# Memory tokens and key weights in eight joint pieces, compressed-value products 512 wide, and a new order table, in a decoder block of sparse attention, mLSTM and memory attention

## The chip, the cores and the metric

The kernel runs on one core of a Trainium2 chip. The metric is the time of one execution on the device in microseconds (us); where several executions were timed it is their median. A profile is one execution, taken by the hardware profiler. The engines are called TensorE (PE in the rows, its weight loads PEld), VectorE (DVE), ScalarE (ACT), GpSimd (POOL) and SyncE (SP, which here only issues DMAs).

## What is computed

One decoder layer on 256 tokens of 1024 features, in fp32. Cut to what matters here:

```
h = rmsnorm(x, g_pre_mix)
z = h @ w_in          # q_nsa, kv_nsa, gates, qkv_ml, if_ml, o_ml, q_mem, g_merge

# sparse attention: compressed, selected and window branches, 4 groups of 4 heads, 64 wide
o_cmp, p_cmp = nsa_compressed(q, k_cmp, v_cmp, ...)   # softmax over 15 compressed blocks
top_i        = nsa_select(p_cmp)
y_nsa = g0 * o_cmp + g1 * nsa_selected(q, k, v, top_i) + g2 * nsa_window(q, k, v)

y_ml  = sigmoid(o_ml) * headnorm(mlstm_chunkwise(...))

# cross attention to 256 memory tokens
kv    = rmsnorm(mem, g_mem) @ w_mem_kv                # 512 key and 512 value columns
y_mem = softmax(q_mem @ k.T * scale) @ v

y = gm0 * (y_nsa @ w_proj_nsa) + gm1 * (y_ml @ w_proj_ml) + gm2 * (y_mem @ w_proj_mem)
x = x + rmsnorm(y @ w_out, g_post_mix)
h = rmsnorm(x, g_pre_ffn)
x = x + rmsnorm((silu(h @ w_gate) * (h @ w_up)) @ w_ffn_down, g_post_ffn)
```

## The kernel before

**Numbers.** An fp32 product is made from three faster ones. Each operand is split in a high half (rounded by a ScalarE copy, `hi`) and a low half (the remainder, by a VectorE subtraction, `lo`); TensorE adds hi·hi, hi·lo and lo·hi in PSUM. The function `split` is this pair. In the rows `whi` and `wlo` are the halves of a weight unit, `hh` holds those of the normed x, `mh` and `ml` those of the memory tokens.

**Weights.** They stream in units of 128x1024 floats (512 KB), each by one DMA from the stacked tensor `W` into one of four `raw` buffers; `fetch` issues the load, `room` takes buffers for the halves (four each), `split` fills them. The program has 161 units. All loads go through SyncE onto one queue, in the order in which they are issued; a load into a `raw` buffer is issued once that buffer's former content has been read.

**The head.** First come the keys of the memory: 1024 features in eight blocks of 128, by 512 key columns. The array `head` holds the gain of the norm (8 columns), the first block of the transposed memory (256), key unit 0 (1024) and the other seven blocks (1792). Four loads of it (`part`, 776, 768, 512 and 1024 columns) fill the tile `memt`; key units 1 to 3 come from `W` between and behind them. `mem_in(k)` makes `mh` and `ml` of block k. Key units 0 to 2 are split in two halves, unit 3 in one (the constant HEAD). For a block TensorE makes 12 matmuls of 256 columns (rows pd<-mh,whi, pd<-ml,whi and pd<-mh,wlo, four each); eight blocks are 96. After that come four value units of the memory (rows pss<-whi,mh and so on, 48 matmuls of 512 columns), and then the units of the sparse attention's keys and values, called kv units here (pss<-hh,whi, hh,whi and hh,wlo in turn, 24 matmuls of 256 columns each). Before the kv units x must be there: VectorE scales the transposed x (`xt`, eight blocks, loaded in two halves), ScalarE copies the high halves `hh`, VectorE subtracts for the low ones. ScalarE also takes the sums of squares of xN and memN (rows xn and mn); from them come 1/rms, made on GpSimd, and its spread over the partitions by the small matmuls rbc<-cs,rr (for x) and rbc<-cs,rm (for the memory).

**The sparse attention** runs in eight halves (four groups by two blocks of 128 tokens), function `nsa_half`, interleaved with the projections that follow. In each half the compressed probabilities of four heads are transposed together (`ptc`), split (`ch` on ScalarE, `cl` on VectorE), and spread by GpSimd into two tiles `ce` of 128x512, one from `ch`, one from `cl`, which are zero outside each head's own 32 rows. TensorE then multiplies `vcs`, the compressed values, with `ce`, in two pairs of heads with two halves each: four matmuls of 256 columns (L1285 to L1288), added to the sum `pvn`.

**What sets the order.** Every engine call is recorded in a `Plan` and issued at the end. `choose` computes for each operation a rank (how late it may come) with the planner's own costs, lays the operations out in time by rank with `schedule`, and issues each engine's instructions in that order. `EARLY` is a table of operation numbers with nanoseconds by which one operation is made more urgent (or, negative, less). Because all instructions are issued in one helper line, every row of the trace says L618.

Of the kernel before, what the change touches and what calls it, by code (L numbers as in the profile page):

```python
# [11 lines left out]
F32 = mybir.dt.float32  # L12
# [6 lines left out]
P = 128  # L19
S = 256  # L20
D = 1024
KD = D // P
# [4 lines left out]
N_UNITS = 161  # L27
HEAD = (2, 2, 2, 1)
# [139 lines left out]
class Plan:  # L168
# [453 lines left out]
def block_kernel(ctx, tc, order, xN, xT, memN, head, cst, vec, row, wg, w1, w2, W, out):  # L622
# [14 lines left out]
    def bigt(tag, bufs, shape, dt, name):  # L637
        return big.tile(shape, dt, tag=tag, bufs=bufs, name=name)
# [32 lines left out]
    ready = {}  # L671
# [108 lines left out]
    mt = bigt("KK", 1, [P, 3080], F32, "memt")  # L780
    part = lambda a, b: dma(out=mt[:, a:b], in_=head[:, a:b])
# [11 lines left out]
    def mem_in(k):  # L793
        gain = mt[:, k:k + 1]
        src = mt[:, 8:264] if k == 0 else mt[:, 1032 + k * S:1288 + k * S]
        if k == 0:
            DVE.tensor_scalar(mh[:, k, :], src, gain, None, op0=ALU.mult)
        else:
            ACT.activation(mh[:, k, :], src, AF.Copy, scale=gain)
        DVE.scalar_tensor_tensor(ml[:, k, :], src, gain, mh[:, k, :].bitcast(F32),  # L800
                                 op0=ALU.mult, op1=ALU.subtract)
# [9 lines left out]
    part(0, 776)  # L811
    part(776, 1544)
    fetch(("mem_k", 1))
    part(1544, 2056)
    fetch(("mem_k", 2))
    part(2056, 3080)
# [4 lines left out]
    for u in range(4):  # L821
        if u and ("mem_k", u) not in ready:
            fetch(("mem_k", u))
        raw = ready.pop(("mem_k", u)) if u else mt[:, 264:1288]
        w = room()
        pieces = HEAD[u]
        for h in range(2):
            if h < pieces:
                c = slice(1024 // pieces * h, 1024 // pieces * (h + 1))
                split(w[0][:, c], w[1][:, c], raw[:, c])  # L830
            mem_in(2 * u + h)
# [389 lines left out]
    def nsa_half(g, tb, qs, yT):  # L1221
# [63 lines left out]
        for pr in range(2):  # L1285
            for i in range(2):
                PE.matmul(pv[:, 2 * pr:2 * pr + 2, :], vcs[:, g, :], ce[i][:, 2 * pr:2 * pr + 2, :],
                          start=False, stop=(pr == 1 and i == 1), skip_group_check=True)  # L1288
# [173 lines left out]
def _layout(inputs):  # L1462
# [79 lines left out]
    head = np.concatenate([a["g_mem"][0].reshape(KD, P).T, memT[:, 0:S], units["mem_k", 0], memT[:, S:]], axis=1)  # L1542
# [33 lines left out]
```

## Time and profile before

| | |
|---|---|
| time, median of 3 runs | 530.76 us (530.58 to 531.57) |
| time of the profiled execution | 530.48 us |
| its span | 528.7 us |
| mean granted clock of TensorE | 0.999 |
| DMA: bytes, mean rate | 97.69 MB, 185 GB/s |
| ScalarE busy | 348.1 us (66%) |
| weight units loaded | 161 x 512 KB, median 4.1 us from issue to landing |

The span reaches from the first to the last instruction in the trace; 1.78 us of the execution lie around it. A row of a timeline has the start, the length, the engine, the operation as out<-in by the program's tile names, the shape, how many instructions it joins, and in brackets how long the engine stood idle ahead of it and what ended that. Lengths of TensorE rows overlap, since matmuls are pipelined: how long one takes in a sequence is read from the distance between starts.

### The profile page before, as it was taken

How to read it: one execution, taken by the hardware profiler on the slowest of the kernel's cores; microseconds unless marked ns; L12 is line 12 of the kernel's file. 1: busy time of each engine (PE TensorE's matmuls, PEld its weight loads, DVE VectorE, ACT ScalarE, POOL GpSimd, SP SyncE). 2: the span in 40 equal slices, each digit the busy share in tenths (PEclk: the TensorE clock that was granted, in tenths of full speed). 3: DMA queues.
4: the chain of work that ended last, by engine and by line, in shares of the span. 5: the costliest groups of instructions: out<-in, count | busy, mean ns of one | idle time of the engine just before them, and what ended most of it. 6: DMA issues, size and time to landing. Idle time of an engine off the chain costs nothing.

```text
span 528.7 us, 9672 instructions
## 1 busy us (share of the span) xinstructions
PE 520.1 (98%) x3536; PEld 479.3 (91%) x3536; DVE 421.5 (80%) x915; ACT 348.1 (66%) x689; POOL 26.0 (5%) x37
## 2 busy tenths in 40 slices
PE   8999999999999999999999999999999999999995
PEld 8899998989899999999999998888888888888884
DVE  5799898799998989998987888966776877754543
ACT  6887977566887968876995446655555655554531
POOL 0000000010002021111110000000000000000000
PEclk9999999999999999999999999999999999999999
DMA  8995465536443181346364766635554665555512
GB/s 310 417 359 213 141 239 160 199 121 197 152 153 139 45 287 69 121 145 215 124 211 145 219 219 209 229 120 170 190 199 166 195 205 191 200 199 195 182 62 79
DMA packets 28703, 97.69 MB, mean 185 GB/s; under 512 B 3312, under 2 KB 5232, under 8 KB 28400
## 3 DMA queue, kind: packets, MB, share of 16 engines
q1 hardware_dynamic: 28656, 97.07, 53.8%
q8 instruction: 28, 0.46, 0.4%
q14 instruction: 19, 0.16, 0.1%
HBM read 94.96 MB, written 1.05 MB: 182 GB/s over the span
## 4 chain that ended last, share of the span: by engine, by line
PE 95%; DMA 1%; ACT 1%; POOL 1%; issue 1%; DVE 0%; SPq 0%; DVEq 0%; ACTq 0%
PE pd L618 49%; PE pss L618 33%; PE pvn L618 3%; PE sc L618 2%; PE ptn L618 2%; DMA raw<-in_W 1%; POOL ce L618 1%; PE ph L618 1%; PE ptx L618 1%; PE psm L618 1%; PE pn L618 1%; PE pvm L618 1%; PE pq L618 1%; PE pgf L618 0%; DVE z L618 0%
## 5 line engine op out<-in xcount | busy, mean ns | idle before, releaser
L618 ACT ACTIVATE whi<-raw 128x1024 fp32r<-128x1024 f32 (+1 forms) x159 | 165.8, 1050 | 119.8 <-PE pss L618 50.6
L618 DVE TENSOR_TENSOR wlo<-raw,whi 128x1024 fp32r<-128x1024 f32 (+1 forms) x159 | 192.1, 1218 | 64.9 <-ACT whi L618 64.1
L618 PE MATMUL pd<-hh,whi 128*128 128x256 f32 x800 | 148.6, 281 | 0.0
L618 PEld LDWEIGHTS pd<-hh,whi 128*128 128x128 f32 x800 | 124.2, 189 | 0.3
L618 PE MATMUL pd<-hh,wlo 128*128 128x256 f32 x400 | 112.2, 280 | 0.0
L618 PEld LDWEIGHTS pd<-hh,wlo 128*128 128x128 f32 x400 | 75.3, 188 | 0.0
L618 PE MATMUL pss<-xc,whi 128*128 128x512 f32 x168 | 43.3, 392 | 0.0
L618 PE MATMUL pss<-whi,u 128*128 128x512 f32 x132 | 42.0, 390 | 0.0
L618 PEld LDWEIGHTS pss<-xc,whi 128*128 128x128 f32 x168 | 30.5, 188 | 5.2
L618 PE MATMUL pd<-xc,whi 128*128 128x512 f32 x120 | 31.5, 392 | 0.0
L618 PE MATMUL pd<-whi,hh 128*128 128x512 f32 x96 | 31.4, 397 | 0.0
L618 DVE CUSTOM_DVE_ANT_0 sc<-sc,msk 128x16 f32<-128x16 f32 (+2 forms) x96 | 27.1, 316 | 4.0 <-PE sc L618 3.7
L618 PEld LDWEIGHTS pss<-whi,u 128*128 128x128 f32 x132 | 24.8, 188 | 5.2
L618 ACT ACTIVATE pp<-sc,mx 128x128 f32<-128x128 f32 (+1 forms) x64 | 26.7, 428 | 0.1
L618 PE MATMUL pss<-wlo,u 128*128 128x512 f32 x66 | 25.7, 389 | 0.0
L618 PEld LDWEIGHTS pd<-xc,whi 128*128 128x128 f32 x120 | 22.0, 188 | 3.7
L618 PEld LDWEIGHTS pss<-xc,wlo 128*128 128x128 f32 x168 | 22.4, 188 | 1.8
L618 PE MATMUL pss<-xc,wlo 128*128 128x256 f32 x168 | 22.6, 277 | 0.0
L618 PEld LDWEIGHTS pd<-whi,hh 128*128 128x128 f32 x96 | 17.7, 188 | 3.2
L618 DVE TENSOR_SCALAR pp<-pp,sm 128x256 f32<-128x256 f32 (+1 forms) x72 | 19.8, 316 | 0.1
L618 ACT ACTIVATE pTh<-ptn 128x512 fp32r<-128x512 f32 x24 | 13.5, 599 | 9.5 <-PE ptn L618 9.5
L618 PE MATMUL pd<-wlo,hh 128*128 128x512 f32 x48 | 18.9, 394 | 0.0
(328 smaller groups left out, 1068.6 us busy)
## 6 DMA issues: line engine op xcount, KB each, us to landing
raw<-in_W SPq DMA_DIRECT2D x161, 512.0 KB, 4.1
w<-in_w SPq DMA_DIRECT2D x2, 1024.0 KB, 8.3
xn<-in_xN SPq DMA_DIRECT2D x2, 512.0 KB, 10.3
mn<-in_memN SPq DMA_DIRECT2D x2, 512.0 KB, 8.7
xt<-in_xT SPq DMA_DIRECT2D x2, 512.0 KB, 8.7
kk<-kk SPq DMA_DIRECT2D x8, 128.0 KB, 3.1
x<-in_xN SPq DMA_DIRECT2D x2, 512.0 KB, 4.1
memt<-in_head SPq DMA_DIRECT2D x1, 512.0 KB, 7.7
```

The lines of the kernel that those rows point to most:

```text
L618: op.ins_ = getattr(op.real, op.method)(*map(arg, op.a), **{k: arg(x) for k, x in op.kw.items()})
```

## The change

Four edits.

1. The head array is laid out in eight pieces of 768 columns, each a block of the transposed memory (256) and the 512 columns of key weights that belong to it. Pieces 0 and 1 go into `memt`, pieces 2 to 7 into `raw` buffers (named `half`). The key units leave `W`: 158 units remain. Every unit is now split in two halves, so unit 3 has one split pair more. The halves stand 16 columns further in their buffers.
2. In `nsa_half` two matmuls of 512 columns take the place of four of 256, 16 in place of 32 in the program.
3. The table `EARLY` is another one, of 139 entries where there were 109; since operations have gone, its numbers stand for other operations than before.
4. N_UNITS follows.

```diff
-N_UNITS = 161
-HEAD = (2, 2, 2, 1)
+N_UNITS = 158
...
     EARLY = """
-    2:14648000 3:2049450 5:2018550 83:28200 145:2300 149:-2050 150:2350 152:5200 153:6450 160:119500 212:14250
...
+    2:32395300 3:4438550 4:838200 5:282400 6:1428950 7:88800 148:4850 149:93250 150:2050 151:2600 152:2050
...
-    mt = bigt("KK", 1, [P, 3080], F32, "memt")
-    part = lambda a, b: dma(out=mt[:, a:b], in_=head[:, a:b])
+    mt = bigt("KK", 1, [P, 1544], F32, "memt")
...
-        src = mt[:, 8:264] if k == 0 else mt[:, 1032 + k * S:1288 + k * S]
+        src = halves[k][:, 0:S]
...
-    part(0, 776)
-    part(776, 1544)
-    fetch(("mem_k", 1))
-    part(1544, 2056)
-    fetch(("mem_k", 2))
-    part(2056, 3080)
+    halves = [mt[:, 8:776], mt[:, 776:1544]]
+    dma(out=mt[:, 0:776], in_=head[:, 0:776])
+    dma(out=mt[:, 776:1544], in_=head[:, 776:1544])
+    for k in range(2, KD):
+        halves.append(wpool.tile([P, 768], F32, tag="raw", bufs=4, name="half"))
+        dma(out=halves[k], in_=head[:, 8 + 768 * k:776 + 768 * k])
...
     for u in range(4):
-        if u and ("mem_k", u) not in ready:
-            fetch(("mem_k", u))
-        raw = ready.pop(("mem_k", u)) if u else mt[:, 264:1288]
-        w = room()
-        pieces = HEAD[u]
+        w = room((16, 16))
         for h in range(2):
-            if h < pieces:
-                c = slice(1024 // pieces * h, 1024 // pieces * (h + 1))
-                split(w[0][:, c], w[1][:, c], raw[:, c])
+            c = slice(512 * h, 512 * h + 512)
+            split(w[0][:, c], w[1][:, c], halves[2 * u + h][:, S:])
             mem_in(2 * u + h)
...
-        for pr in range(2):
-            for i in range(2):
-                PE.matmul(pv[:, 2 * pr:2 * pr + 2, :], vcs[:, g, :], ce[i][:, 2 * pr:2 * pr + 2, :],
-                          start=False, stop=(pr == 1 and i == 1), skip_group_check=True)
+        for i in range(2):
+            PE.matmul(pv, vcs[:, g, :], ce[i], start=False, stop=i == 1, skip_group_check=True)
```

The table moves instructions on all engines. Three places are shown, before and then after; the issuing line is L618 in the kernel before and L620 in the changed one.

**SyncE, the start of the program**: the loads in the order in which they enter the queue (`raw` are weight units, `mn` memN, `xn` x, `xt` its transpose, `vc` and `cs` constants). Before:

```order
L618 DMA memt<-in_head 128x768
L618 DMA memt<-in_head 128x512
L618 DMA raw<-in_W 128x1024 x2
L618 DMA memt<-in_head 128x1024
L618 DMA raw<-in_W 128x1024 x2
L618 DMA xn<-in_xN 128x1024 x2
...
L618 DMA raw<-in_W 128x1024 x2
L618 DMA mn<-in_memN 128x1024
L618 DMA xt<-in_xT 128x1024
L618 DMA raw<-in_W 128x1024 x2
L618 DMA mn<-in_memN 128x1024
L618 DMA xt<-in_xT 128x1024
```

After:

```order
L620 DMA memt<-in_head 128x776
L620 DMA memt<-in_head 128x768
L620 DMA half<-in_head 128x768 x4
L620 DMA xn<-in_xN 128x1024
L620 DMA half<-in_head 128x768 x2
L620 DMA raw<-in_W 128x1024 x2
L620 DMA xn<-in_xN 128x1024
L620 DMA vc<-in_vec 128x80
L620 DMA cs<-in_cst 128x128
L620 DMA raw<-in_W 128x1024 x3
L620 DMA xt<-in_xT 128x1024 x2
L620 DMA mn<-in_memN 128x1024 x2
```

The first half of x now stands between the pieces, and the first kv unit (the last of `raw` x3) ahead of both transposed halves of x and of memN; the second kv unit comes after them.

**ScalarE and VectorE, from the memory's value units to the second kv unit.** Before, first ScalarE from the second pair of value units on, then VectorE there:

```order
L618 ACTIVATE whi<-raw 128x1024 x2
L618 ACTIVATE mn,sums<-mn 128x1024
L618 ACTIVATE hh<-xt 128x256 x4
L618 ACTIVATE whi<-raw 128x1024 x2
L618 ACTIVATE mn,sums<-mn 128x1024
L618 ACTIVATE hh<-xt 128x256 x4
L618 ACTIVATE whi<-raw 128x1024 x2
```

```order
L618 SCALAR_TENSOR_TENSOR xt<-xt,vc,rbc 128x256 x4
L618 TENSOR_TENSOR hh<-xt,hh 128x256 x4
L618 TENSOR_TENSOR wlo<-raw,whi 128x1024 x2
L618 TENSOR_SCALAR rv<-sums 128x2
L618 SCALAR_TENSOR_TENSOR xt<-xt,vc,rbc 128x256 x4
L618 TENSOR_TENSOR hh<-xt,hh 128x256 x4
L618 COPY rmb<-rbc 128x256
L618 TENSOR_TENSOR wlo<-raw,whi 128x1024
```

After, the same two:

```order
L620 ACTIVATE whi<-raw 128x1024 x3
L620 ACTIVATE hh<-xt 128x256 x7
L620 ACTIVATE mn,sums<-mn 128x1024
L620 ACTIVATE hh<-xt 128x256
L620 ACTIVATE mn,sums<-mn 128x1024
L620 ACTIVATE whi<-raw 128x1024 x2
```

```order
L620 TENSOR_TENSOR wlo<-raw,whi 128x1024 x3
L620 SCALAR_TENSOR_TENSOR xt<-xt,vc,rbc 128x256 x8
L620 TENSOR_TENSOR hh<-xt,hh 128x256 x8
L620 TENSOR_SCALAR rv<-sums 128x2
L620 TENSOR_TENSOR wlo<-raw,whi 128x1024
L620 COPY rmb<-rbc 128x256
```

The eight blocks of x and both sums of memN now stand in one run between the splits of the first kv unit (the last of x3) and of the second. On TensorE the four rbc<-cs,rm matmuls have moved from ahead of the first kv unit to behind it.

**VectorE behind `cl` in the seventh half of the sparse attention** (`sc` and `mx` are its scores and their maxima). Before:

```order
L618 TENSOR_TENSOR cl<-ptc,ch 128x128
L618 ISA sc,mx<-sc,msk 128x256
L618 ISA mx 128x1
L618 ISA sc,mx<-sc,msk 128x16
L618 ISA mx 128x1
L618 ISA sc,mx<-sc,msk 128x256
```

After:

```order
L620 TENSOR_TENSOR cl<-ptc,ch 128x128
L620 ISA sc,mx<-sc,msk 128x256
L620 ISA mx 128x1
L620 TENSOR_TENSOR wlo<-raw,whi 128x1024
L620 ISA sc,mx<-sc,msk 128x16
L620 ISA mx 128x1
```

A weight split now comes third here. Of the eight halves such a split stands within a few rows behind `cl` in the second, fourth, sixth and last in the kernel before, and in the seventh as well in the changed one.

More of the change, by code (lines that the diff above doesn't have):

```diff
@@ L1541, in _layout @@
     memT = ft(a["mem"][0].T).reshape(P, KD * S)
-    head = np.concatenate([a["g_mem"][0].reshape(KD, P).T, memT[:, 0:S], units["mem_k", 0], memT[:, S:]], axis=1)
+    head = np.concatenate([a["g_mem"][0].reshape(KD, P).T] + [
+        x for k in range(KD) for x in (memT[:, k * S:k * S + S], units["mem_k", k // 2][:, 512 * (k % 2):512 * (k % 2) + 512])],
+        axis=1)
     arrs = {"xN": a["x"][0], "xT": xT, "memN": a["mem"][0], "head": head, "cst": cst, "vec": vec, "row": row, "wg": wg, "w1": w1, "w2": w2}
```

23 rows, old and new, of the table EARLY are left out of this document.

## The prediction

> **What bounds the kernel now.** I began with the page's engine rows, its clock row and its chain of waits.
>
> ```profile
> span 528.7 us, 9672 instructions
> PE 520.1 (98%) x3536; PEld 479.3 (91%) x3536; DVE 421.5 (80%) x915; ACT 348.1 (66%) x689; POOL 26.0 (5%) x37
> PEclk9999999999999999999999999999999999999999
> PE 95%; DMA 1%; ACT 1%; POOL 1%; issue 1%; DVE 0%; SPq 0%; DVEq 0%; ACTq 0%
> ```
>
> TensorE is busy for 520.1 of 528.7 us at an unthrottled clock, and 95% of the chain that ends last is TensorE's own. So the change can gain only where TensorE stands (8.6 us in all, start and tail included) or by making its matmuls fewer or quicker, and it can lose wherever another engine comes late. Next I read the table of stretches (busy time of PE, PEld, DVE, ACT, POOL, then granted clock, DMA share, GB/s).
>
> ```profile
> 5.00:6.00 1.00, 1.00 (x10) 1.00 (x10) 0.91 (x3) 0.95 (x2) 0.00 (x0) 1.00 0.97 147
> 8.00:9.00 1.00, 0.01 (x1) 0.01 (x1) 0.03 (x1) 0.69 (x2) 0.00 (x0) 1.00 0.95 389
> 9.00:27.00 18.00, 18.00 (x115) 16.46 (x116) 14.37 (x25) 15.35 (x25) 0.71 (x1) 1.00 1.03 417
> 27.00:47.00 20.00, 20.00 (x156) 19.28 (x155) 19.46 (x35) 16.70 (x27) 0.70 (x1) 1.00 0.92 338
> ```
>
> TensorE stands idle for one whole microsecond of the head (8 to 9), and not at all from 9 to 47. From 27 to 47 VectorE is busy for 19.46 of 20 us, so there a little more or later work on VectorE would be felt. The queue runs at 417 GB/s in the head, except from 5 to 6, where the first bytes of the big weight tensor come (147). The chain (start, length, what) and TensorE's timeline (start, length, in brackets the idle time ahead) tell what ends the head's wait.
>
> ```profile
> 2.11 6.17 DMA raw<-in_W
> 8.99 8.89 PE pd L618 x72
> 35.37 5.65 PE pd L618 x48
> 64.89 8.50 PE pd L618 x75
> ...
> 7.30 0.64 PE L618 MATMUL pd<-mh,wlo 128*128 128x256 f32 x4
> 8.99 0.74 PE L618 MATMUL pd<-mh,whi 128*128 128x256 f32 x4 [1.05 <-ACT whi L618]
> 9.57 0.64 PE L618 MATMUL pd<-ml,whi 128*128 128x256 f32 x4
> 10.04 0.64 PE L618 MATMUL pd<-mh,wlo 128*128 128x256 f32 x4
> 17.72 0.40 PE L618 MATMUL pss<-whi,mh 128*128 128x512 f32 x1
> 29.11 0.61 PE L618 MATMUL rbc<-cs,rm 128*128 128x128 f32 x4
> 29.47 0.48 PE L618 MATMUL pss<-hh,whi 128*128 128x256 f32 x2
> ```
>
> The second key unit of the memory lands at 2.11 + 6.17 = 8.28 us. Once ScalarE has made its high half, TensorE goes on at 8.99, after 24 of its 96 key products.
>
> **The joint pieces: −1.30 us.** Each piece carries one block of memory tokens and the key weights that go with it, 128x768 floats or 0.39 MB. When do the pieces come, and can the engines keep up?
>
> ```profile
> 3.93 0.63 ACT L618 ACTIVATE whi<-memt 128x512 fp32r<-128x512 f32 x1 [1.29 <-DMA memt<-in_head]
> 4.92 0.51 ACT L618 ACTIVATE mh<-memt 128x256 fp32r<-128x256 f32 x1 [0.35 <-DMA memt<-in_head]
> ...
> 4.72 0.68 DVE L618 TENSOR_TENSOR wlo<-memt,whi 128x512 fp32r<-128x512 f32 x1
> 5.46 0.48 DVE L618 SCALAR_TENSOR_TENSOR ml<-memt,mh 128x256 fp32r<-128x256 f32 x1
> ```
>
> Pieces 0 and 1 are as large as the loads that landed at 3.93 and 4.92, so a piece comes every 0.99 us: piece 2 at 5.9, piece 5 at 8.9. The first half of xN, 0.52 MB, stands ahead of piece 6 and takes 1.26 us at 417 GB/s. Pieces 6 and 7 also wait for buffers that the splits of pieces 2 and 3 leave, so they come at about 11 and 12.5. A piece costs ScalarE 0.63 + 0.51 = 1.14 us and VectorE 0.68 + 0.48 = 1.16; TensorE needs 12 matmuls, three steps of 0.48 us (9.57 to 10.04), or 1.44. TensorE is the slowest of the four, starts piece 2 at 7.30 + 0.48 = 7.78 and piece 6 at 13.5: piece 2 landed 1.9 us before and piece 6 about 2.5 before, and a split takes 1.3 (0.63 + 0.68). So it runs on. The 72 matmuls are 18 steps of 0.48, to 7.78 + 8.64 = 16.42, where before they ended at 17.72: −1.30, which is the 1.05 of idle time and the slower restart. Bounds: −1.05, when only the idle time goes, and −1.78, when the matmuls run at the quicker of two paces that the chain shows for the same shape (8.50/75 = 0.113 us, against 5.65/48 = 0.118 and 0.48/4 = 0.12). The two added split instructions (the last unit in two) lie in the margin of 0.3 us that ScalarE and VectorE have per piece. The slow first bytes of the weight tensor now stand ahead of the first value unit, at 12 to 13, and cost (417 − 147)/417 = 0.65 us there. TensorE wants that unit at 16.4; it lands near 12.5 + 0.65 + 1.26 = 14.4 and its split, about 2.3 us, ends at 16.7. TensorE takes the high half first and is nearly half a microsecond in by then: wait 0, at most 0.5.
>
> **A new wait at the second kv unit: +0.30 us.** Being 1.30 ahead helps at the end only if later data is early too. The new order puts the splits of x ahead of it: xt 8 times and hh 8 times on VectorE, and the sums over both halves of memN on ScalarE, all between the first kv unit and the second.
>
> ```profile
> 20.48 1.06 ACT L618 ACTIVATE mn<-mn 128x1024 f32<-128x1024 f32 x1 [0.17 <-DMA mn<-in_memN]
> 21.45 0.18 ACT L618 ACTIVATION_READ_ACCUMULATOR mn<-mn 128x1 f32 x1
> 27.72 1.59 ACT L618 ACTIVATE hh<-xt 128x256 fp32r<-128x256 f32 x4 [0.90 <-DVE xt L618]
> ...
> 20.35 1.23 DVE L618 TENSOR_TENSOR wlo<-raw,whi 128x1024 fp32r<-128x1024 f32 x1 [0.62 <-ACT whi L618]
> 27.21 1.65 DVE L618 SCALAR_TENSOR_TENSOR xt<-xt,vc,rbc 128x256 f32<-128x256 f32 x4
> 28.78 1.42 DVE L618 TENSOR_TENSOR hh<-xt,hh 128x256 fp32r<-128x256 f32 x4
> ...
> 32.38 0.40 PE L618 MATMUL pss<-hh,whi 128*128 128x256 f32 x2
> 32.62 0.28 PE L618 MATMUL pss<-hh,wlo 128*128 128x256 f32 x1
> ```
>
> When TensorE wants it: the value products take 29.11 − 17.72 = 11.39, so the first kv unit starts at 27.81, lasts 32.38 − 29.47 = 2.9, then come the 4 rbc matmuls, now here (29.47 − 29.11 = 0.36), and one step of 0.24 (32.38 to 32.62) to the first product with the low half: 31.3. When it is ready: up to the first kv unit the queue carries eight pieces (3.15 MB), xN (1.05), the small constants (0.1) and five units (2.62), 6.92 MB in all; what follows piece 0, landed at 3.93, takes 6.52/0.417 = 15.6 us, plus the 0.65 and up to 1 for buffers: 20.2 to 21.2. Its split ends 2.3 later, 22.5 to 23.5. Eight xt, 0.39 apart, end at 25.7 to 26.7. ScalarE's seventh hh follows, then sum (1.15), hh (0.4), sum (1.15), and the high half (1.06): 29.5 to 30.5. VectorE's eight hh end at 28.5 to 29.6, the low half (1.23) at 30.7 to 31.7. The wait is 0 to 0.4, and up to 0.7 with an estimated 0.1 us for each of three hand-overs between engines; I take 0.30, near the middle. Behind that split VectorE holds rmb, kt and the next low half; they would shift by the same 0.3, and since TensorE shifted too, nothing more is lost.
>
> The row of 417 GB/s carries all of this. A page of the Trainium skill speaks against it ("DMA: Bandwidth & Descriptors", section "Where 436 GB/s comes from"): for transfers between HBM and SBUF the HBM side, about 358 GB/s, binds. The row of 9 to 27 us, at 417, disagrees; by that rule the second kv unit would be ready near an estimated 33.4, and the sum an estimated 531.2.
>
> **Products 512 wide: −0.05 us.** 32 matmuls become 16 of double width.
>
> ```profile
> 18.42 0.40 PE L618 MATMUL pss<-whi,mh 128*128 128x512 f32 x1
> 18.65 0.39 PE L618 MATMUL pss<-wlo,mh 128*128 128x512 f32 x1
> ```
>
> One of 512 columns follows the last after 0.23, two of 256 take 2 × 0.113 to 2 × 0.118: at most 16 × 0.006 = 0.1 is gained, at least 0. I take 0.05. In either form the last products of a half wait for the same second ce, so this part alone takes no wait away.
>
> **The new order from 48 us on: 0, from −0.4 to +0.9.** TensorE's instructions and their durations stay; only waits can change. The two of before stand behind GpSimd.
>
> ```profile
> 159.16 1.04 POOL L618 TENSOR_TENSOR ce<-ch,cs 128x512 fp32r<-128x512 f32 x1 [26.51 <-ACT ch L618]
> 160.17 2.03 POOL L618 TENSOR_TENSOR ce<-cl,cs 128x512 fp32r<-128x512 f32 x1
> ...
> 159.37 1.93 DVE L618 TENSOR_TENSOR wlo<-raw,whi 128x1024 fp32r<-128x1024 f32 x1
> ...
> 162.25 0.62 PE L618 MATMUL pvn<-ce,vcs 128*128 128x256 f32 x3 [0.16 <-POOL ce L618]
> 213.11 0.61 PE L618 MATMUL pvn<-ce,vcs 128*128 128x256 f32 x3 [0.23 <-POOL ce L618]
> ```
>
> Beside GpSimd's ce a weight split on VectorE takes 1.93 instead of 1.23, and a ce beside a split 2.03 instead of 1.04. In the order of before such a split follows `cl` closely in four of the eight halves (the second, fourth, sixth and last), in the new order in five (the seventh as well). Only two of the four cost TensorE a wait: elsewhere enough other matmuls stand ahead of the product. So the two waits may go (−0.16 − 0.23 = −0.39), or all five halves wait, and one more with them, 0.23 and a slow restart each (+0.9). I take 0.
>
> The Trainium skill ("Advanced Engine Details and Errata", VectorE Performance Modes) says that VectorE's second SBUF port is shared with GpSimd and that two-port VectorE instructions and GpSimd's block each other. These rows agree, for instructions with two SBUF inputs. By that rule alone, five slow halves at the 0.2 of before, the sum would be an estimated 530.1.
>
> **The pace of the matmuls**: 0.113 and 0.118 for one shape differ by 4.4 ns; over some 1,200 such products that is 5.3 us, and a new order may move a tenth of them: ±0.5, taken as 0. **The tail**: the last of z is 256 columns wider, so that the last load out is 256 KB, not 128; both take 2.0 to 2.1 us to land.
>
> ```profile
> out<-z SPq DMA_DIRECT2D x2, 256.0 KB, 2.0
> out<-z SPq DMA_DIRECT2D x4, 128.0 KB, 2.1
> ```
>
> I take 0, at most +0.3.
>
> **The sum**, against the profiled execution (528.7 of span and 1.78 around it, 530.48; the median of the runs is 0.28 above): 530.48 − 1.30 + 0.30 − 0.05 = 529.43, say **529.4**. A measurement of this kernel tells about 0.2%, or 1.06 us, from no change, so "faster" begins near 529.42, just at the forecast.
>
> **The rivals.**
> *More is gained* (under 528.6, chance 0.15): no wait at the second kv unit, the quicker pace in the key products, and no waits for ce: 530.48 − 1.78 − 0.39 − 0.05 = 528.3, down to 527.8 with the pace elsewhere. For it: the pace 0.113 is usual later. Against it: VectorE has little room until 47 us.
> *The gain is taken back later* (530.2 to 531.5, chance 0.20): the pieces come as said, but the second kv unit is ready at 32.0 (wait 0.7) and two more ce waits come (0.46): 530.48 − 1.30 + 0.70 − 0.05 + 0.46 = 530.3. If the pieces came no earlier than the unit of before, and TensorE waited at 8 us as now, it would be 530.4.
> *Slower* (over 531.54, chance 0.10), by one mechanism: the split of the second kv unit stands behind both sums over memN, so a queue that runs slower than 417 holds it. With xT, memN and itself that unit ends 6.92 + 2.62 = 9.54 MB down the queue. At the 338 GB/s of the row of 27 to 47 us it lands at 3.93 + 9.14/0.338 + 1.65 = 32.6, its low half ends at 34.9, and the wait is 3.6: 530.48 − 1.30 + 3.6 − 0.05 = 532.7. It decides from about 353 GB/s down, where the wait passes 2.4, the gain and 1.06 together. For it: the row with 338. Against it: that stretch is limited by when buffers come free, and the bytes in question moved at 417.
>
> **Chances and range.** The forecast, 528.6 to 530.2, has 0.55; 0.35 of it lies under 529.42, since without the new wait, which may well be 0, the sum is 529.1, and 0.20 above. With the rivals: faster 0.35 + 0.15 = 0.50, the same 0.20 + 0.20 = 0.40, slower 0.10. The range goes from 527.8 (most of the larger gain) to 531.2 (530.48 − 1.05 + 0.7 + 0.9 = 531.0, and a little of the pace); it leaves out the slower case and the edges of the others.
>
> **What will show it.** Right: no idle time of TensorE between 5 and 16 us; the first value product near 16.4, the first kv product near 27.8; the low GB/s of 5 to 6 moved to 12 to 13; a wait of 0 to 0.7 ahead of the first product with the second kv unit's low half, near 31; sixteen pvn<-ce of 512 columns; ce of 2.0 in up to five halves. Wrong: TensorE waiting inside the pieces, the first kv product later than 28.5, a wait over 1 us near 31, VectorE late again before 48 us, or a span that differs though no wait does, which would be the pace.

## The result, and the profile after

The change made the kernel slower: 534.53 us (median of 4 runs, 534.38 to 535.07), beside 531.16 us for the kernel before, measured alongside. The ratio is 1.0063, with a 95% interval of 1.0045 to 1.0082, so about 3.4 us were lost where the forecast had a gain of about 1.1 (from 530.48 to 529.4); its range ended at 531.2. The profiled execution of the changed kernel has a span of 532.4 us, 3.7 more than before.

The page of the changed kernel, its span, the engines' busy time and the chain by engine:

```profile
span 532.4 us, 9634 instructions
PE 522.1 (98%) x3520; PEld 479.2 (90%) x3520; DVE 420.0 (79%) x916; ACT 347.4 (65%) x689; POOL 29.0 (5%) x37
PE 91%; DMA 3%; ACT 2%; DVE 2%; POOL 1%; issue 1%; SPq 0%; DVEq 0%; ACTq 0%
```

TensorE's share of the chain fell from 95% to 91%, and what took its place is loads, ScalarE and VectorE: TensorE now waits. The table of stretches says where (the columns are those of the prediction), first for the changed kernel, then two stretches of the kernel before that were not shown yet.

```profile
5.00:6.00 1.00, 1.00 (x5) 1.00 (x6) 0.87 (x2) 0.96 (x2) 0.00 (x0) 1.00 1.03 298
8.00:9.00 1.00, 1.00 (x11) 1.00 (x10) 0.25 (x2) 0.77 (x2) 0.00 (x0) 1.00 1.02 412
11.00:14.00 3.00, 3.00 (x27) 3.00 (x27) 1.89 (x4) 2.26 (x5) 0.00 (x0) 1.00 0.79 185
9.00:27.00 18.00, 16.95 (x107) 14.76 (x107) 11.16 (x18) 11.74 (x18) 0.70 (x1) 1.00 0.94 334
27.00:47.00 20.00, 19.15 (x140) 17.55 (x138) 19.15 (x39) 17.54 (x32) 0.70 (x1) 1.00 0.90 349
140.00:160.00 20.00, 18.67 (x117) 16.39 (x116) 19.09 (x38) 16.16 (x25) 4.23 (x2) 1.00 0.46 151
```

```profile
11.00:14.00 3.00, 3.00 (x28) 3.00 (x26) 2.55 (x6) 3.00 (x6) 0.00 (x0) 1.00 1.02 418
140.00:160.00 20.00, 20.00 (x150) 18.64 (x148) 19.04 (x39) 17.52 (x28) 0.83 (x1) 1.00 0.48 158
```

The idle microsecond at 8 to 9 is gone, as the change meant. But TensorE stands for 1.05 us between 9 and 27, for 0.85 between 27 and 47, where before it stood not at all, and for 1.33 between 140 and 160. From 11 to 14 us the queue moved 185 GB/s where it had moved 418, and over 9 to 27 us 334 instead of 417. In those three microseconds the DMA engines were still busy for 0.79 of the time (the column ahead of the GB/s; 1.02 before). At the rate of before that share would have moved an estimated 320 GB/s (418 × 0.79/1.02), so two things were lost: for a fifth of the time there was nothing to move, and what moved was slow. TensorE's timeline of the changed kernel names what each wait was for:

```profile
4.78 1.22 PE L620 MATMUL pd<-mh,whi 128*128 128x256 f32 x4
5.80 0.95 PE L620 MATMUL pd<-ml,whi 128*128 128x256 f32 x4
6.59 0.64 PE L620 MATMUL pd<-mh,wlo 128*128 128x256 f32 x4
...
16.24 0.74 PE L620 MATMUL pd<-mh,whi 128*128 128x256 f32 x4 [0.53 <-ACT mh L620]
19.30 0.50 PE L620 MATMUL pss<-wlo,mh 128*128 128x512 f32 x1 [0.53 <-DVE wlo L620]
31.01 0.40 PE L620 MATMUL pss<-hh,whi 128*128 128x256 f32 x1 [0.38 <-DVE hh L620]
33.02 0.38 PE L620 MATMUL pss<-hh,whi 128*128 128x256 f32 x1 [0.36 <-DVE hh L620]
157.42 0.50 PE L620 MATMUL pvn<-ce,vcs 128*128 128x512 f32 x1 [1.33 <-POOL ce L620]
```

So there are two places: the head, up to about 36 us, and one product of the sparse attention at 157 us. The chain of the changed kernel gives the size of the first:

```profile
2.12 6.09 DMA half<-in_head
...
10.01 5.12 DMA half<-in_head
...
19.27 5.79 DMA raw<-in_W
...
33.07 0.96 ACT whi L620
...
34.05 1.24 DVE wlo L620
...
35.33 2.78 PE pss L620 x22
38.11 5.44 PE pd L620 x48
```

The block of 48 matmuls behind the first two kv units starts at 38.11, where it started at 35.37 before: 2.74 us lost in the head. At the second place 1.33 is waited instead of 0.16 + 0.23 at two such places before: 0.94. Together that is 3.68 of the 3.7 by which the span grew. That it comes out so evenly is partly luck, since smaller differences of both signs stand beside it (this block takes 5.44 instead of 5.65, and the tail is 0.2 shorter).

The three long loads in the chain are piece 3, piece 7 and the first kv unit. Piece 3 was issued at once and met a slow moment of the queue that the kernel before has too: there the second key unit landed at 8.28. Why the other two came late is in SyncE's timeline (start, length from the first issue to the last, count), the changed kernel first:

```profile
8.18 2.16 SPq L620 DMA_DIRECT2D half<-in_head  x2
11.01 1.32 SPq L620 DMA_DIRECT2D raw<-in_W  x2
12.39 0.42 SPq L620 DMA_DIRECT2D xn<-in_xN  x1
...
14.41 5.19 SPq L620 DMA_DIRECT2D raw<-in_W  x3
19.65 0.90 SPq L620 DMA_DIRECT2D xt<-in_xT  x2
```

```profile
3.54 0.92 SPq L618 DMA_DIRECT2D raw<-in_W  x2
4.50 1.32 SPq L618 DMA_DIRECT2D xn<-in_xN  x2
```

In the kernel before, the third key unit, the first value unit and both halves of xN were on their way by 5.8 us. In the changed one SyncE stands at piece 6 until 8.18 and at piece 7 until 10.01, since four raw buffers hold pieces 2 to 5 and each must be split first. The value units, the second half of xN, the transposed x and memN are queued behind, and the queue has too little under way. On top of the late issue the load itself was slow: piece 7 took 5.12 us from issue to landing, while the very first load of the program, of almost the same size and with nothing ahead of it, took 3.3. Why it was slow is not shown.

### The profile page after: what moved, and what is told of

It reads as the page before. It is cut to its first block, busy times and chain, and to the rows that moved or that the text cites. A ratio compares the mean times of both kernels' runs of the same rounds, so it can differ in the third digit from the quotient of the medians.

```text
span 532.4 us, 9634 instructions
## 1 busy us (share of the span) xinstructions
PE 522.1 (98%) x3520; PEld 479.2 (90%) x3520; DVE 420.0 (79%) x916; ACT 347.4 (65%) x689; POOL 29.0 (5%) x37
## 3 DMA queue, kind: packets, MB, share of 16 engines
HBM read 94.96 MB, written 1.05 MB: 180 GB/s over the span
## 4 chain that ended last, share of the span: by engine, by line
PE 91%; DMA 3%; ACT 2%; DVE 2%; POOL 1%; issue 1%; SPq 0%; DVEq 0%; ACTq 0%
PE pd L620 49%; PE pss L620 30%; PE pvn L620 3%; DMA half<-in_head 2%; PE sc L620 2%; PE ptn L620 2%; POOL ce L620 1%; DMA raw<-in_W 1%; ACT whi L620 1%; DVE wlo L620 1%; PE ph L620 1%; PE ptx L620 1%; PE pn L620 1%; PE pvm L620 1%; PE psm L620 1%
## 5 line engine op out<-in xcount | busy, mean ns | idle before, releaser
L620 DVE TENSOR_TENSOR wlo<-raw,whi 128x1024 fp32r<-128x1024 f32 x154 | 187.8, 1224 | 72.4 <-ACT whi L620 72.0
L620 ACT ACTIVATE whi<-raw 128x1024 fp32r<-128x1024 f32 x154 | 163.1, 1061 | 117.9 <-PE pd L620 52.1
L620 PE MATMUL pd<-hh,whi 128*128 128x256 f32 x800 | 148.9, 281 | 0.0
L620 PEld LDWEIGHTS pd<-hh,whi 128*128 128x128 f32 x800 | 124.5, 189 | 0.5
L620 PE MATMUL pd<-hh,wlo 128*128 128x256 f32 x400 | 111.7, 280 | 0.0
L620 PEld LDWEIGHTS pd<-hh,wlo 128*128 128x128 f32 x400 | 75.2, 188 | 0.2
L620 PE MATMUL pss<-xc,whi 128*128 128x512 f32 x168 | 43.4, 392 | 0.0
L620 PE MATMUL pss<-whi,u 128*128 128x512 f32 x132 | 42.1, 390 | 0.0
L620 PEld LDWEIGHTS pss<-xc,whi 128*128 128x128 f32 x168 | 30.7, 188 | 5.3
L620 PE MATMUL pd<-whi,hh 128*128 128x512 f32 x96 | 32.1, 397 | 0.0
L620 PE MATMUL pd<-xc,whi 128*128 128x512 f32 x120 | 31.8, 392 | 0.0
L620 DVE CUSTOM_DVE_ANT_0 sc<-sc,msk 128x16 f32<-128x16 f32 (+2 forms) x96 | 27.1, 320 | 4.4 <-PE sc L620 3.9
L620 PEld LDWEIGHTS pss<-whi,u 128*128 128x128 f32 x132 | 24.8, 188 | 5.2
L620 ACT ACTIVATE pp<-sc,mx 128x128 f32<-128x128 f32 (+1 forms) x64 | 26.8, 428 | 1.8 <-PE ptn L620 1.4
L620 PE MATMUL pss<-wlo,u 128*128 128x512 f32 x66 | 25.7, 389 | 0.0
L620 PEld LDWEIGHTS pd<-xc,whi 128*128 128x128 f32 x120 | 22.0, 188 | 3.7
L620 PEld LDWEIGHTS pss<-xc,wlo 128*128 128x128 f32 x168 | 22.3, 188 | 1.8
L620 PE MATMUL pss<-xc,wlo 128*128 128x256 f32 x168 | 22.6, 277 | 0.0
L620 PEld LDWEIGHTS pd<-whi,hh 128*128 128x128 f32 x96 | 17.8, 188 | 3.2
L620 DVE TENSOR_SCALAR pp<-pp,sm 128x256 f32<-128x256 f32 (+1 forms) x72 | 19.9, 319 | 0.1
L620 PE MATMUL pd<-wlo,hh 128*128 128x512 f32 x48 | 19.1, 398 | 0.0
L620 ACT ACTIVATE pTh<-ptn 128x512 fp32r<-128x512 f32 x24 | 13.6, 598 | 8.1 <-PE ptn L620 8.0
```

What stands on the lines that cost most here:

```text
L620: op.ins_ = getattr(op.real, op.method)(*map(arg, op.a), **{k: arg(x) for k, x in op.kw.items()})
```

## The experiments

Each experiment takes the order of instructions on every engine from a named kernel, as a written list in place of the planner's table (the list also says which buffer each tile takes), so that one part can be changed without moving the others; what is moved on purpose is said with the run. The ratios to the kernel before (95% intervals), with the medians in us:

| run | what it is | median | ratio |
|---|---|---|---|
| the change | pieces, wide products, new order | 534.53 | 1.0063 (1.0045 to 1.0082) |
| before_512 | wide products alone | 529.39 | 0.9971 (0.9960 to 0.9981) |
| table_only | wide products, new order | 531.97 | 1.0015 (1.0005 to 1.0025) |
| pieces_only | wide products, pieces | 531.99 | 1.0018 (1.0008 to 1.0027) |
| wide_memt | the change, no piece waits for a buffer | 532.83 | 1.0037 (1.0024 to 1.0050) |
| wide_old | pieces_only, no piece waits for a buffer | 530.70 | 0.9994 (0.9984 to 1.0004) |
| roomy_old | wide_old, and the first two value units don't wait either | 529.26 | 0.9966 (0.9952 to 0.9979) |
| roomy_v1 | roomy_old, and the second value unit ahead of xN | 529.31 | 0.9970 (0.9957 to 0.9982) |
| ce_later | the change, two splits moved | 533.91 | 1.0057 (1.0042 to 1.0072) |
| ce_one | the change, one split moved | 534.19 | 1.0052 (1.0035 to 1.0070) |
| warm_9 | the change, nine warm-up products | 534.10 | 1.0062 (1.0043 to 1.0081) |
| last_wide | wide product in the last half alone | 531.03 | 1.0003 (0.9994 to 1.0012) |
| seven_wide | wide products in the other seven | 529.58 | 0.9973 (0.9963 to 0.9983) |

The kernel before had medians of 530.89 to 531.16 in these comparisons; ratios are compared below, not medians of different comparisons.

**The parts of the change, one by one.** The wide products alone, in the order of before:

> The kernel before with the products of the compressed values 512 wide and nothing else: all other instructions in the order of before, the first wide product at the place of the first narrow one, the second at that of the second. Theory (the wide products cost nothing and gain at most 0.1): 530.4 to 531.3, not to be told from before. Rival (the wide product costs, since TensorE's second wait for ce then holds a longer product): over 531.8.

Neither: 0.9971, a gain of about 1.5 us where 0.05 was forecast. Compared matmul by matmul, the two traces agree within 0.25 us up to 225 us; then before_512 falls behind by up to 0.37, is level at 280 us and from there on ahead, by more with every block, until it is 1.38 ahead at 322. Two rows of the chain, first of the kernel before, then of before_512, with start, length, and the count of matmuls, the same ones in both:

```profile
293.98 11.31 PE pss L618 x96
305.29 5.65 PE pd L618 x48
```

```profile
293.46 10.88 PE pss L747 x96
304.34 5.44 PE pd L747 x48
```

The same 48 matmuls take 5.65 in one and 5.44 in the other: 0.1177 against 0.1133 each, the two paces of the prediction. Some 300 matmuls from 280 to 320 us run at the quicker one, 300 x 0.0044 = 1.3 us. To see whether the products save or the pace does, two runs split them:

```diff
+        if (g, tb) == (3, 1):
+            for i in range(2):
+                PE.matmul(pv, vcs[:, g, :], ce[i], start=False, stop=i == 1, skip_group_check=True)
+        else:
-        for pr in range(2):
+            for pr in range(2):
...
```

> The kernel before with the 512-wide products in the last of the eight halves of the sparse attention only (two matmuls in place of four at one place of the program); order of before otherwise. Theory (the 1.5 us that before_512 gained are not the products themselves but the pace of the some 300 matmuls of 256 columns from 280 to 320 us, which goes from 0.118 to 0.1135 when the two last products are wide): pace 0.1135 there, 529.4 to 530.0, that is 1.0 to 1.5 under before. Rival (each wide product saves by itself): an eighth of the gain, within 0.3 of before.

> The reverse of last_wide: wide products in the first seven halves, narrow ones in the last. Theory (pace after the last half): 0.118 from 280 to 320, within 0.4 of before, 530.5 to 531.3. Rival (each wide product saves): seven eighths of the gain of before_512, 529.5 to 529.8.

The times went to the rival in both: 1.0003 with the last half alone, 0.9973 with the other seven. But the place of the saving did not. First last_wide, then seven_wide, the same rows of the chain:

```profile
294.88 11.31 PE pss L748 x96
306.18 5.65 PE pd L748 x48
```

```profile
292.50 10.88 PE pss L747 x96
303.38 5.44 PE pd L747 x48
```

The time follows the pace behind the sparse attention, as the theory said, and no product saves where it stands; but what sets that pace lies in the first seven halves, not in the last. Which of them it is was not tried. The written lists of these two runs put every tile into the same buffer, so which buffers the tiles take is not what sets it.

Then the order and the pieces, each without the other:

> The order of the changed kernel with the head of before: key units loaded as before (memt of 3080 columns, units 1 to 3 from W), products 512 wide, everything behind the memory's keys in the order of the changed kernel. Against before_512 (529.4) it differs by the new order alone, against the changed kernel (534.5) by the joint pieces alone. Theory (the pieces cost by their buffers, the table costs by the ce of 3.23 us and by the slow pace that it keeps from 280 to 320 us): loads run ahead again, first kv product near 28.9 (as before less the 0.36 of rbc), at most 0.5 of waits at the kv units; wait of 1.3 for ce; pace 0.118 from 280 to 320; 531.8 to 532.8. Rival (the whole loss is the table's): 534 or more. Rival (the whole loss is the pieces'): 529.0 to 530.0.

> The joint pieces of the change (memt of 1544 columns, six pieces in raw buffers), products 512 wide, and everything behind the memory's keys in the order of before. The first pieces are split in the order of the changed kernel, the loads of x stand behind all eight pieces as in before. Theory (two pieces and every load that is queued behind them on SyncE wait for one of four raw buffers): piece 7 near 14.5 to 15, both halves of xN behind it, near 17.5 and 19; TensorE waits for value units or for hh; first kv product at 30.5 to 32, and 531.5 to 533.0. TensorE's order behind the head is that of before_512, so the pace from 280 to 320 is 0.1135 if that order sets it. Rival (the pieces help as forecast): 528.0 to 529.0.

The two costs add up. Against before_512 (0.9971) the order alone adds 0.0044, the pieces alone 0.0047; the sum gives 1.0062, and the whole change has 1.0063 (the intervals, 0.001 to 0.002 either way, are wider than this agreement). In us these are about 2.3 and 2.5. Both were tried with wide products only. With the table alone the head is sound: the trace of table_only has no wait of TensorE from 9 us until this product, and then the pace is the slow one (one row of its timeline, then two of its chain).

```profile
154.66 0.50 PE L746 MATMUL pvn<-ce,vcs 128*128 128x512 f32 x1 [1.33 <-POOL ce L746]
```

```profile
295.10 11.31 PE pss L746 x96
306.40 5.65 PE pd L746 x48
```

So the table's 2.3 are some 1 us at that product and 1.3 of pace that before_512 had won. With the pieces alone everything is in the head. TensorE's waits in pieces_only:

```profile
15.81 0.73 PE L746 MATMUL pd<-mh,whi 128*128 128x256 f32 x4 [1.03 <-ACT mh L746]
18.44 0.50 PE L746 MATMUL pss<-wlo,mh 128*128 128x512 f32 x1 [0.46 <-DVE wlo L746]
21.54 0.71 PE L746 MATMUL rbc<-cs,rr 128*128 128x128 f32 x4 [0.30 <-POOL rr L746]
23.22 0.50 PE L746 MATMUL pss<-wlo,mh 128*128 128x512 f32 x1 [0.50 <-DVE wlo L746]
```

The last piece, a value unit, 1/rms of x and another value unit come late in turn: 2.3 us of waits, and a slow restart behind each, in place of the one wait of 0.93 that before_512 has at 9 us. TensorE's pace behind the sparse attention was the quick one here, with TensorE's order of before_512: the order behind the head sets it, not the head.

**Room for the pieces.** Pieces 2 and 3 in the old, wider memt, the order of the changed kernel kept:

```diff
-    mt = bigt("KK", 1, [P, 1544], F32, "memt")
+    mt = bigt("KK", 1, [P, 3080], F32, "memt")
...
-    halves = [mt[:, 8:776], mt[:, 776:1544]]
+    halves = [mt[:, 8 + 768 * k:776 + 768 * k] for k in range(4)]
...
     for k in range(2, KD):
-        halves.append(wpool.tile([P, 768], F32, tag="raw", bufs=4, name="half"))
+        if k > 3:
+            halves.append(wpool.tile([P, 768], F32, tag="raw", bufs=4, name="half"))
```

> The changed kernel with pieces 2 and 3 in a memt tile of its old width (3080), so that only pieces 4 to 7 take raw buffers and none of the pieces waits for a buffer; order of all instructions as in the changed kernel. Theory A (the joint pieces took the room of the old memt away: two pieces and every unit behind them are issued only when a buffer of four comes free, which is what delays piece 7 to 15.1 and the first kv unit to 25.1): piece 7 lands at 12.5 to 13.5, the first kv product starts near 28.7 instead of 30.35, the waits at the first and second kv unit shrink, and 534.5 becomes 532.5 to 533.2. Rival B (the loads are slow in themselves, the packets of pieces 6 and 7 took up to 1.85 us): piece 7 still lands after 14.5 and the time stays within 0.5 of 534.5. Rival C (the new order around the kv units sets the end): piece 7 comes early, the first kv product too, but TensorE waits as much more at the second kv unit, 534.0 to 534.5.

Theory A: 1.0037 instead of 1.0063. Piece 7 landed at 13.2 and the first kv product started at 28.94 instead of 30.35. Its trace keeps a wait at the value units and one at the kv units:

```profile
17.72 0.50 PE L902 MATMUL pss<-wlo,mh 128*128 128x512 f32 x1 [0.53 <-DVE wlo L902]
31.18 0.38 PE L902 MATMUL pss<-hh,whi 128*128 128x256 f32 x1 [0.36 <-DVE hh L902]
```

The same with the order of before, and then with two more pieces in the space of the tile for memN:

> As pieces_only, but with memt at its old width of 3080 columns for pieces 0 to 3, so that no piece waits for a buffer. Theory: piece 7 near 12.5, TensorE runs through the pieces and reaches the first value product near 16.5 (17.8 in before_512); the first value unit still waits for the buffer of piece 4 (about 10.6) and holds the loads of x behind it, so 0.5 to 0.7 of wait there; 528.3 to 529.3. Pace from 280 to 320 as in before_512. Rival (the order of before has no use for an earlier start, the wait moves whole to the kv units): 529.2 to 529.8.

> As wide_old, with pieces 4 and 5 in the space of the tile for memN, which is loaded later, so that only pieces 6 and 7 take raw buffers and the first two value units are issued without a wait. Theory (buffers are what the pieces lack): no gap of the queue before 20 us, piece 7 near 12, first value unit near 13.5, no wait of TensorE from 5 us to the kv units; 528.0 to 528.9, faster than before_512 by 0.5 to 1.4. Rival: as wide_old within 0.3.

```diff
+    mu = bigt("C", 1, [P, 1536], F32, "memu")
-    halves = [mt[:, 8 + 768 * k:776 + 768 * k] for k in range(4)]
+    halves = [mt[:, 8 + 768 * k:776 + 768 * k] for k in range(4)] + [mu[:, 0:768], mu[:, 768:1536]]
...
-        if k > 3:
+        if k > 5:
```

From pieces_only to wide_old to roomy_old the ratio falls from 1.0018 to 0.9994 to 0.9966: each buffer that the pieces don't take from the units behind them gives time back, 2.8 us in all. But roomy_old only reaches before_512 (0.9971, intervals overlapping), short of the gain that was expected, and wide_old (530.70) came out later than its theory and its rival both had it. So in the order of before, room is what the loss hung on, but it buys no gain. Roomy_old waits for the second value unit; with that load moved ahead of xN, for xN. One row of each, roomy_old first, then roomy_v1:

> As roomy_old, with the load of the second value unit ahead of both halves of xN on SyncE's queue. Theory (in roomy_old the pieces bring TensorE to the value products 1.3 us earlier, but the second unit lands at 18.3 and the gain is waited away there, 0.63 at 20.8): the unit lands near 15.5, that wait goes, 528.4 to 529.0. Rival (xN now comes too late, rbc and hh wait instead): the wait moves to rbc<-cs,rr or to the first kv product, 529.0 to 529.6.

```profile
20.81 0.50 PE L746 MATMUL pss<-wlo,mh 128*128 128x512 f32 x1 [0.46 <-DVE wlo L746]
```

```profile
20.10 0.71 PE L746 MATMUL rbc<-cs,rr 128*128 128x128 f32 x4 [0.88 <-POOL rr L746]
```

The rival was right: the wait moves from one load to the other. TensorE starts the value products earlier and then stands for the next load. An earlier start of the keys was worth next to nothing, since what follows came no earlier: here the loads bound the head. Where the loads themselves come earlier, the gain stays. The head of seven_wide is that of before, but in its trace the second key unit landed at 7.83 instead of 8.28; TensorE went on at 8.54 instead of 8.99, and the block of 48 began at 34.91 instead of 35.37.

**The product at 157 us.** GpSimd's second ce and VectorE beside it, in the changed kernel:

```profile
154.13 3.23 POOL L620 TENSOR_TENSOR ce<-cl,cs 128x512 fp32r<-128x512 f32 x1
...
154.10 2.37 DVE L620 TENSOR_TENSOR wlo<-raw,whi 128x1024 fp32r<-128x1024 f32 x2
```

VectorE's two splits run at their own speed (1.2 each). Ce starts with them and ends 0.9 us after the second (157.36 against 156.47), as if nearly all of its own 1.04 us had been done behind them. In the row order of VectorE, ce_later moves both, ce_one the second:

```diff
 TENSOR_TENSOR cl<-ptc,ch
 COPY on<-pd
-TENSOR_TENSOR wlo<-raw,whi x2
 TENSOR_TENSOR on<-on,rw
+TENSOR_TENSOR wlo<-raw,whi x2
```

> The changed kernel with two weight splits of VectorE (the two that stood side by side behind cl in the second half of the sparse attention) moved behind the next row on<-on,rw, and the load that reuses their raw buffer moved with them; nothing else. Theory (the pair held GpSimd's second ce for 3.23 us, and TensorE waited 1.33 for it): that ce takes 1.04 to 1.1, the wait goes, 534.5 becomes 533.1 to 533.3. Rival (the product was late anyway, or VectorE comes late elsewhere for its 2.4 us of lost time): the ce is short but a new wait of TensorE before 180 us takes over half or more of it, 533.8 to 534.6. The head is untouched, so this run also shows whether piece 7 lands at 15.1 again or whether that was one slow load: a landing under 14 would say the latter.

> The changed kernel with only the second of the two neighbouring weight splits behind cl (second half of the sparse attention) moved behind on<-on,rw; one split stays beside GpSimd's second ce. Theory (one split holds a ce for 1 us, a pair for 2.2): that ce takes 2.03 instead of 3.23, TensorE waits 0.2 to 0.3 for it instead of 1.33, the later wait of ce_later at pq (0.65) stays or shrinks, 533.2 to 533.9. Rival (GpSimd's ce waits for as long as VectorE works from SBUF, whatever the count): still above 2.8, and 534.3 or more.

GpSimd and TensorE, in ce_later and then in ce_one:

```profile
153.87 1.04 POOL L745 TENSOR_TENSOR ce<-cl,cs 128x512 fp32r<-128x512 f32 x1
...
161.36 0.39 PE L745 MATMUL pq<-qkm 128*128 128x256 f32 x1 [0.43 <-DVE dw L745]
```

```profile
155.21 2.09 POOL L745 TENSOR_TENSOR ce<-cl,cs 128x512 fp32r<-128x512 f32 x1
...
157.36 0.50 PE L745 MATMUL pvn<-ce,vcs 128*128 128x512 f32 x1 [0.20 <-POOL ce L745]
```

One split holds ce for 1 us, two for 2.2. Without them the 1.33 go, but VectorE lost the time in which it now waits and is late 7 us on (0.43 at pq). Between 153 and 165 us the trace of ce_later wins 0.9 us on that of the change, and the trace of ce_one 1.3. Little of it is seen in the times: 533.91 and 534.19 are above what the theories had (533.1 to 533.3, and 533.2 to 533.9), and 1.0057 and 1.0052 lie inside the interval of the change. The head differs from run to run by as much (in the profiled execution of ce_one it waited 1.8 us for hh, in that of the change 0.7). So the mechanism is shown by its rows, and its price in the whole only roughly.

**The start.** In the changed kernel the first eight products took 1.81 us, from the start of the first at 4.78 to that of the ninth at 6.59. Before it was 1.24.

> The changed kernel with nine warm-up products instead of eight, so that TensorE has no gap of 0.2 us between the last warm-up product and the first key product; order as in the changed kernel. Theory C1 (that gap put off the full clock from 5.07 to 6.50 us): full clock from about 5.1, eight half-speed products of 0.213 become four or fewer, the time falls by 0.3 to 0.6, unless the wait for piece 7 swallows it (then the second and third piece start earlier by 0.4 and the time stays). Theory C2 (when the full clock comes varies by itself): it comes at some other time, with no relation to the gap, and the time stays within 0.3 of the changed kernel.

The ratio is 1.0062, the same as that of the change, and the first eight took 1.15. Four traces with one and the same head (before, before_512, last_wide, seven_wide) have 1.24, 1.42, 1.82 and 1.66, so this varies by itself, as theory C2 says. What varies is the moment of the full clock: the traces' own records of it begin at 5.07, 5.51, 6.52 and 5.95 us in these four, at 6.50 in the changed kernel and at 5.16 in warm_9. (The clock column of the stretches counts the time ahead of the first record as full.) In the changed kernel products ahead of that moment start 0.213 us apart, and 0.117 to 0.120 behind it. Whether a ninth product helps as well can't be told from one trace, and how much of this scatter reaches the end of the kernel is not shown.

## Why the prediction was wrong

**What bounds the kernel** was read rightly: only TensorE's waits and pace moved the time. So was the wait at 8 to 9 us, which is gone in the changed kernel.

**The pieces (−1.30 forecast, about +2.5 measured).** The step that failed is the sentence that pieces 6 and 7 "come at about 11 and 12.5", with the buffers as a side remark. They came at 12.3 and 15.1, and the first value unit at 16.8 instead of 14.4. In the five traces with the narrow memt piece 7 landed between 14.3 and 15.1, so it is no accident of one run; with the wide one it landed at 13.2 (wide_memt) and 11.5 (wide_old). The working allowed at most 1 us for buffers. What it did not count: memt gave up 1536 columns, 0.79 MB of room for loads in flight, or 1.9 us of the queue; the four raw buffers had to replace it; and every load behind a waiting one on SyncE waits too, xN and the transposed x among them, which need no raw buffer. The arithmetic of the pieces themselves held. In roomy_v1, where neither the pieces nor the first two value units wait for a buffer, the first value product stands at 16.3 (forecast: 16.4). Even there the first kv product started at 29.49, against 29.58 in before_512: the second premise, that an earlier start of the keys is passed on, failed as well.

**The first kv unit (20.2 to 21.2 forecast).** It landed at 25.1 (in table_only, with the old head, at 21.4). The row of 417 GB/s was carried over from a kernel whose loads never waited to one whose loads do. The rival "slower" named this condition, a queue under 353 GB/s, and the row of 9 to 27 us has 334. It gave it a chance of 0.10, argued against by the very 417, and put its price at the second kv unit; most of the waiting came earlier, at piece 7, the first value unit and hh. As a forecast of the loads it was good all the same: it had the second kv unit landed at 32.6 and its low half done at 34.9, and 31.9 and 35.3 were measured; the head lost 2.74 where its sum was 2.2 above the kernel before.

**The wait at the second kv unit (+0.30).** It came, and by the forecast mechanism: in the chain ScalarE makes the high half at 33.07, behind both sums over memN, although the unit had landed at 31.9, and TensorE takes up the low half at 35.33. That is 0.59 us after its first product with this unit (34.74); in table_only the same two starts lie 0.32 apart (32.31 and 32.63), so 0.27 was lost. With the new order alone there was thus no wait; the order is harmless there until the loads come late. That the size is near +0.30 is luck, since TensorE and the unit were both some 4 us later than forecast.

**The wide products (−0.05).** The term was sized by the products themselves, and these save nothing to speak of. The pace of what follows was a term of its own, taken as 0 with ±0.5. In the order of before the wide products moved it by 1.3 to 1.5 us, which no step of the prediction had. In the new order it stayed as it was in the kernel before (11.31 for the 96 matmuls in the change, 309.16 − 297.85, and in table_only), so the change as a whole won nothing by it. The new order with narrow products was not run.

**The order from 48 us on (0, from −0.4 to +0.9).** Against the kernel before, the waits for ce came to +0.94, just above the upper end. The step was the price of 0.23 for a half with a split near `cl`, taken from halves with one split. In the second half the new order has two splits in a row: the wait is 1.33. Held ce (over 1.2 us) stand in six halves of the changed kernel's trace, and only this one cost more than 0.3. Against before_512 the new order costs about 2.3; what goes beyond the wait is the pace that the wide products won in the order of before and not in the new one.

**The rules from the Trainium skill.** The rule of the Trainium skill on VectorE and GpSimd ("Advanced Engine Details and Errata", VectorE Performance Modes) agreed again in its direction, for instructions with two SBUF inputs. The estimate made from it did not come, and its terms give 530.0, not the 530.1 that stands there. The 358 GB/s of the Trainium skill ("DMA: Bandwidth & Descriptors", "Where 436 GB/s comes from") were not what bound the queue: it moved 412 GB/s from 8 to 9 us, and its slow stretch from 11 to 14 us came with late issues and with loads that were slow for a reason not shown.

**The tail and the median** moved nothing: from the last matmul to the end of the span it is 6.4 us, before 6.6.

## What to carry to other kernels

Before an array is moved into buffers that others use, count how many loads can be in flight before the first one must wait, and which loads that need no buffer stand behind that one on the same queue; the rate of a queue that never waited says nothing of one that does. A wait that is removed at the start pays only if the next load is also early. And a split of the change into its parts (a two by two of order and layout here) told more than the sum: the parts added up within their intervals, and the wide products, which were thought to be worth nothing, were the one part worth keeping, in the order of before.

## What the runs showed of the hardware

- TensorE has two paces for the same 256-column matmuls, 0.1133 and 0.1177 us. They hold for long stretches. In the order of before, making earlier products wide switches the pace of some 300 matmuls further on (in seven_wide the last wide product stands at 258.7 us, the 300 from 280 to 320); in the new order the slow pace stood there with wide products too. Runs with the same order behind the head agreed there (pieces_only, wide_old, roomy_old and roomy_v1 with before_512). What the switch is stays open.
- GpSimd's tensor_tensor of 1.04 us is held while VectorE runs weight splits, instructions with two SBUF inputs, without a pause: it took 2.09 beside one split and 3.23 beside two, and ended 0.9 us after the last of them.
- The slow moment of the queue near 5 to 8 us is not that of the weight tensor, as the prediction had it: in the changed kernel no byte of W is under way by then, and piece 3 still landed 1.8 us behind piece 2, where 1.0 is usual. Such moments come later too, and where no piece waits for a buffer: in roomy_old piece 7 landed at 12.5, 1.7 us behind piece 6. The cause is open.
- TensorE's full clock starts at a moment that varies between executions: the records of it begin between 4.5 and 7.1 us in the fourteen traces, and the first eight products took 1.0 to 1.9 us. The Trainium skill ("TensorE: Matmul & The Clock Gate", Part 1) says that the window which decides this runs freely and that the phase at kernel start varies; these rows agree with it.
